# Placing the residual's border scale in the second mixing block, and later places for its side steps in TensorE's written order

## The chip, the core and the metric

The kernel runs on one core of one Trainium2 chip. The metric is the device time of one execution in microseconds, the median over runs. TensorE (PE in the profile) multiplies, VectorE (DVE) and GpSimd (POOL) do elementwise work, ScalarE (ACT) evaluates functions and issues part of the DMAs, SyncE (SP) issues the rest of them.

## What is computed

Two models run one after the other over 512 tokens of width 1024, two layers each. Block 1 has latent attention, indexed sparse attention, retention and a squared-ReLU network; block 2 has a gated delta rule (GDN), a native sparse attention with three branches (NSA), a stick-breaking attention, a convolved gated network and a gated embedding. Between them stands a border: the output of block 1 is `rmsnorm(x, g_final)`, and that is at once the residual of block 2 and the input of block 2's first norm. Cut to this:

```python
x = first_block(...)            # ends with: return rmsnorm(x, g_final)
h = x                           # second_block
for i in range(2):
    hn = rmsnorm_2(h, ln_mix[i])
    mix = concatenate([o_gdn, head_rmsnorm(o_nsa), head_rmsnorm(o_sb)])
    h = h + mix @ w_out[i]
    h = h + conv_ffn(rmsnorm_2(h, ln_ffn[i]), ...)
    h = h + sigmoid(rmsnorm_2(h, ln_ple[i]) @ w_ple_gate[i]) * rmsnorm_2(p[i] @ w_ple[i], ple_norm[i])
return rmsnorm_2(h, ln_final)
```

## The kernel before, in words

The residual x is kept in eight tiles of 128 features by 512 tokens (`x[k]`). Each float32 product is made as three products of a high and a low part (`mm3`, `mm3t`, line 382), so that weights are split after loading into `whi` (ACT, line 278) and `wlo` (DVE, line 279), and activations into `hi` and `lo`.

**TensorE's order is written out ahead.** While the program is built, `drive` keeps a plan clock `pe["t"]` that counts columns over 2400, in microseconds. A main thread (projections and output products) and side threads (attention heads, transposes, the delta rule, norms) yield lags: `yield 3.92` or `after(lag, "s")` means that the thread's next step isn't placed before so much plan time has passed and, for `after`, before a PSUM bank of that kind counts as free. When no thread is due, the plan clock jumps; on the chip nothing is waited for on that account, only the order is kept. `mark(name, lag)` sets a time from which `until(name)` holds. A side step that is due goes ahead of the main thread as the shares (`SHARE`) allow. PSUM banks of kind "s" (in block 2's mixing five, numbers 2 to 6) go round in strict rotation, those of kind "g" (two) likewise. The order on the other engines comes from the compiler's schedule, in which a step written earlier goes first where both are ready.

**Mixing of block 2** (`block2_mix`, line 1330). `norm` (line 1338) sums the squares over TensorE and makes the token scales `r`, then `rb`, their broadcast. The main thread goes through projections `kz`, the three feature projections of the delta rule (`delta(j)`, each three tiles, `post_g` at 1479), and the token projections between them; then `z`, `sq`, `sk`, `sv`. `post_g` convolves on DVE, transposes (`conv`), normalises q and k heads into `ghat` on POOL, and transposes these back (line 1515). `gdn_inverse` (line 1537) makes the 64x64 triangular systems: products kT kT, a product with `dts` on DVE into `lt`, transposes of `lt`, and DMAs through DRAM (`lsc`, `tsc`) from SP's queue; `gdn_solve` and `gdn_scan` follow. `keys` and `queries` turn NSA's keys and queries (`kwr`, `nq`) into high and low halves; `compress` makes the compressed keys and values from a "g" bank that its tail (`chid`) frees. `nsa` runs 48 heads in four workers; its result is transposed by `mix_features` (tile `on`), which ends in a mark from which the main thread takes up `out_proj(mixa)`. `breaking` (line 1990) makes the halves of `sq` and `sk` (tiles `q`, `k`, `kl`) and then runs the stick-breaking heads, whose first step (`weigh`) is products of `k` and `kl` with `q`.

**The residual in the mixing.** `put_away` writes the eight tiles of x to DRAM from ACT's queue, `fetch` reads them back ahead of `out_proj`, whose `post` adds to `x[m]`. In the first layer (`st["acc2"]` is there) `norm` also makes `rf`, the border norm's token scale; it broadcasts it (`rbf`), waits for the mark `dts`, and multiplies the eight tiles on DVE ahead of `put_away` (lines 1363 to 1368), the first of them behind the gates' last step (`steps[0]`).

In block 1's mixing the diff touches two lags: the one ahead of the indexer's scores (`qst`, line 924) and the mark of the rotated query part (`qr`, line 1029), from which `mla_queries` takes it up.

Of the kernel before, what the change touches and what calls it, by code (L numbers as in the profile page):

```python
# [9 lines left out]
F = mybir.dt.float32  # L10
# [279 lines left out]
def build(ctx, tc, a, out, off, stages=99):  # L290
# [550 lines left out]
    def block1_mix(l, st, nxt):  # L841
# [47 lines left out]
        def indexing():  # L889
            yield until("mi")  # L890
            yield after(0, "t")
            kst = sl([128, S], "kst", dt=R)
            tp = ps("t")
            for b in range(4):
                tr(tp[0:96, blk(b)], kx[b // 2][:, b % 2, 0:96])
            act(kst[0:96], tp[0:96])
            yield after(0, "t")
            kd.extend(key_halves([kx[b // 2][:, b % 2, 160:224] for b in range(4)], 1))
            yield after(0, "t")
            tp = ps("t")  # L900
            for b in range(4):
                tr(tp[0:32, blk(b)], kx[b // 2][:, b % 2, 128:160])
            act(krt[64:96], tp[0:32])
            mark("krt", 1.0)
            for b in (3, 2, 1):

                src = heads(qi[b // 2][:, b % 2], 8)
                hi = tmp([128, 8, 32], "qih", dt=R)
                act(hi, src)
                part = [tmp([128, 4, 3, 32], "qp") for _ in range(2)]  # L910
                for j in range(2):
                    z = slice(4 * j, 4 * j + 4)
                    nc.gpsimd.tensor_copy(out=part[j][:, :, 0:2], in_=hi[:, z].unsqueeze(2).to_broadcast([128, 4, 2, 32]))
                    tt(part[j][:, :, 2], src[:, z], hi[:, z], ALU.subtract)
                yield 4.75
                qst = []
                for j in range(2):
                    yield after(0, "t")
                    tp = ps("t")
                    for h in range(4):  # L920
                        tr(tp[0:96, blk(h)], part[j][:, h].rearrange("p t d -> p (t d)"))
                    qst.append(sl([128, S], "qst", dt=R))
                    act(qst[j][0:96], tp[0:96])
                yield after(0.98, "s")
                n = 128 * (b + 1)
                acc = None
                for h in range(8):
                    sp = ps("s")
                    mm(sp[:, 0:n], qst[h // 4][0:96, blk(h % 4)], kst[0:96, 0:n])
                    e = tmp([128, n], "rel")  # L930
                    act(e, sp[:, 0:n], ACTF.Relu)
                    new = tmp([128, n], "acc")
                    if acc is None:
                        ts(new, e, wi[:, b, h:h + 1], 0.0, ALU.mult, ALU.add)
                    else:
                        stt(new, e, wi[:, b, h:h + 1], acc, ALU.mult, ALU.add)
                    acc = new
                    yield after(0.36 + 0.2 * b, "s")
                begin(top(b, acc), 0)
                yield until(f"mask{b}")  # L940
# [78 lines left out]
        for c in range(3):  # L1019
            def post_q(b, p, c=c):  # L1020
                if c < 2:
                    act(qn[b][:, 256 * c:256 * c + 256], p[:, 0:256], scale=rq_[:, b:b + 1])
                else:
                    act(qr[b], p[:, 0:256], scale=rq_[:, b:b + 1])
                    rope(heads(qr[b], 8), heads(qr[b], 8), 8, 32, rope32, b)

            yield from token_proj(cq, 256, post_q, kt=6, need="rq_")
            if c:
                mark("qn" if c == 1 else "qr", 1.0 if c == 1 else 4.5)
        vm, kn, kT = [None] * 4, [None] * 4, []  # L1030

        def mla_keys():
# [297 lines left out]
    def block2_mix(l, st, nxt, shared):  # L1330
# [3 lines left out]
        r = const.tile([128, 4], F, tag="rmix", name="rmix")  # L1334
        r8 = const.tile([128, 4], F, tag="r8", name="r8")
        rb = sl([128, S], "rb")

        def norm():
            yield 3.92
            if st["acc2"] is None:  # L1340
                with tc.high_priority():
                    rms_cols(st["acc"], D, r)
                mark("r")
                ts(r8, r, 0.125)
                put_away()
            else:

                with tc.high_priority():
                    rf = rms_cols(st["acc"], D)
                    v = ty([128, 4], "border")  # L1350
                    stt(v, col_sums(st["acc2"]), 1.0 / D, rf, ALU.mult, ALU.mult)
                    tt(v, v, rf, ALU.mult)
                    ts(v, v, EPS, op0=ALU.add)
                    pow_half(v, v, 4)
                    tt(r, v, rf, ALU.mult)
                mark("r")
                ts(r8, r, 0.125)
            yield NR
            with tc.high_priority():
                bcast(r, rb)  # L1360
            mark("rb")
            if st["acc2"] is not None:
                rbf = bcast(rf)
                yield until("dts")
                for k in range(8):
                    ins = stt(x[k], x[k], P("g_final")[:, k:k + 1], rbf, ALU.mult, ALU.mult).ins
                    tc.add_manual_dep(ins, steps[0], NOSYNC, reason="the gates first")
                put_away()

        begin(norm(), 0)  # L1370
# [6 lines left out]
        beta, sig = gb("beta"), gb("sig", 18)  # L1377
        eG, eR, bG = gb("eG"), gb("eR"), gb("bG")
        eT = const.tile([128, 3, 4, 2], F, tag="eT", name="eT")
        dts, steps = [], []  # L1380

        ab = const.tile([128, 4, 30], F, tag="ab", name="ab")

        def gates():
# [37 lines left out]
            act(eG, p[:, 0:24].rearrange("p (b h) -> p b h", b=4), ACTF.Exp)  # L1422
            act(eR, p[:, 24:48].rearrange("p (b h) -> p b h", b=4), ACTF.Exp)
            act(eT.rearrange("p j b c -> p (j b c)"), p[:, 48:72], ACTF.Exp)
            steps.append(tt(bG, beta, eG, ALU.mult).ins.name)

            for h in range(6):
                tgs = [None, None]
# [50 lines left out]
        def post_g(i, p):  # L1479
# [21 lines left out]
            if what == 2:  # L1501
                for hh in range(2):
                    tt(B[2 * j + hh][:, :, 0:64], t4[:, :, hh], beta[:, :, 2 * j + hh:2 * j + hh + 1].to_broadcast([128, 4, 64]), ALU.mult)
            else:
                sq, t = tmp([128, 4, 2, 64], "gsq"), tmp([128, 4, 2, 64], "ghat")
                act(sq.rearrange("p b h d -> p (b h d)"), tp, ACTF.Square)
                act(t.rearrange("p b h d -> p (b h d)"), tp)
                n = ty([128, 4, 2], "gn")
                reduce(n, sq, ALU.add)
                ts(n, n, EPS, op0=ALU.add)  # L1510
                pow_half(n, n, 8)
                if what == 0:
                    ts(n, n, 0.125)
                gt(t, t, n.unsqueeze(3).to_broadcast([128, 4, 2, 64]), ALU.mult)
                yield after(PG[1], "t")
                (qT if what == 0 else kT)[j] = transposed([flat(t, b) for b in range(4)])
                if what == 0:
                    gt(t, t, per_token(eG, j, 64), ALU.mult)
                    yield after(2.0, "t")
                    WQ[j] = sl([128, 4, 2, 2, 64], "wq", "wq")  # L1520
                    tp = ps("t")
                    for b in range(4):
                        tr(tp[:, blk(b)], flat(t, b))
                    t4 = tp.rearrange("p (b c t) -> p b c t", b=4, c=2)
                    for ch in range(2):
                        act(WQ[j][:, :, ch, 1 - ch], t4[:, :, ch])
                else:
                    for hh in range(2):
                        h = 2 * j + hh
                        KA[h] = sl([128, 4, 2, 64], "KA")  # L1530
                        gt(KA[h][:, :, hh], t[:, :, hh], eR[:, :, h:h + 1].to_broadcast([128, 4, 64]), ALU.mult)
                        gt(B[h][:, :, 64:128], t[:, :, hh], bG[:, :, h:h + 1].to_broadcast([128, 4, 64]), ALU.mult)
# [4 lines left out]
        def gdn_inverse(j):  # L1537

            lt, L, T = [], [], []
            for hh in range(2):  # L1540
# [5 lines left out]
                    mm(p[:, blk(b)], kT[j][zz, blk(b)], kT[j][zz, blk(b)])  # L1546
                lt.append(tmp([128, S], "lt"))
                tt(lt[hh], p, dts[h], ALU.mult)
            yield 1.0
            for hh in range(2):  # L1550
                h = 2 * j + hh
                yield after(0, "t")
# [140 lines left out]
        def compress(kind):  # L1693
# [11 lines left out]
                    if c % 2:  # L1705
                        yield
            begin(compress_out(kind, p))
            room[0] = pe["t"] + 3.0

        def compress_out(kind, p):  # L1710
            hid, th = tmp([128, 128], "chid"), tmp([128, 128], "cth")
# [49 lines left out]
            roped(nq[0][:, b], b, p[:, 128:256], r8[:, b:b + 1])  # L1761

        yield from token_proj(xx, 256, post_v2)
        spawn(keys("kw", kwr), 9.05)
        spawn(queries(0), 16.9)
        yield from delta(2)
        spawn(compress_blocks(kcr, "k"), until("kc"), 0)
# [24 lines left out]
        def mix_features(o, i):  # L1792
            for k in range(3):
                yield after(0, "t")
                mixa[3 * i + k] = to_features([o[b][:, 2 * k:2 * k + 2].rearrange("p h d -> p (h d)") for b in range(4)], mixn[:, i:i + 1])
            mark(f"mix{i}", 2.28)

        def gdn_scan():
            yield until("rules")
# [129 lines left out]

        def sparse():  # L1930
            yield until("ks", "kw", "nq0", "nq1", "nq2", "vs", "cmp_k", "cmp_v")
            crew(LIVE[2], nsa(), "nsa", lag=8.62)
            yield until("nsa")
            yield from mix_features(on, 1)

# [70 lines left out]
            mark("mixb", 1.5)  # L2006

        begin(breaking())
        yield until("mix0", "mix1")
        fetch()  # L2010
        share(SHARE[4])
        yield from out_proj(mixa)
        yield until("mixb")
# [181 lines left out]
```

## Time and profile before

| | |
|---|---|
| median of 3 runs | 3048.47 us (3047.78 to 3053.13) |
| the profiled execution's own time | 3049.75 us |
| its span, first to last instruction | 3048.0 us |
| busy: PE, PEld, DVE, ACT, POOL | 97%, 81%, 62%, 45%, 23% of the span |
| mean granted clock of TensorE | 0.988 of full speed |
| DMA | 259.38 MB, mean 85 GB/s |

PE is TensorE's matmuls, PEld its weight loads, which lie beside them. A line of a wait names the instruction that stood still, what it waited for, the sum, how often and the longest. A line of a stretch has the length, then each engine's busy time with the number of instructions, the granted clock (1.00 is 2.4 GHz, 0.50 is 1.2 GHz), the DMAs' share and GB/s.

### The profile page before, as it was taken

To read this page: it belongs to the slowest core of one execution; us is meant where nothing else is said; L and a number is where in the kernel's file an instruction comes from. 1 tells how busy PE (TensorE), PEld (TensorE's weight loads), DVE (VectorE), ACT (ScalarE), POOL (GpSimd) and SP (SyncE) were. 2 spreads that over 40 slices of the span, in tenths; PEclk is the share of its full clock that TensorE was granted. 3 is DMA by queue.
4 is the path that set the end of the run, shared out by engine and by line. 5 is a ranking of instruction groups with operands and counts; after the bars stand their busy time and mean duration, and the time that the engine had idled before them with its cause. 6 is when DMAs were issued, how large, how long until landed. Compare 5 with 4: busy or idle time off the path is not lost.

```text
span 3048.0 us, 46930 instructions
## 1 busy us (share of the span) xinstructions
PE 2962.5 (97%) x18306; PEld 2472.4 (81%) x18306; DVE 1889.6 (62%) x3432; ACT 1360.6 (45%) x2536; POOL 713.6 (23%) x874
## 2 busy tenths in 40 slices
PE   8999999999999999998999999999999999999998
PEld 7888888888887888887898778887788987788876
DVE  6858444447858434457866675655778666755556
ACT  5644422244645332254455543334454565533343
POOL 4211311123201211145313120003454131200024
PEclk9999999999999999999999999999999999999999
DMA  4211223332122333322310222232323102222322
GB/s 135 77 62 58 86 94 97 97 117 84 64 77 73 97 92 95 97 92 91 89 58 24 82 91 94 92 106 90 115 78 87 60 24 80 92 92 94 106 90 76
DMA packets 105790, 259.38 MB, mean 85 GB/s; under 512 B 21728, under 2 KB 40032, under 8 KB 105568
## 3 DMA queue, kind: packets, MB, share of 16 engines
q1 hardware_dynamic: 97504, 241.70, 25.3%
q10 hardware_dynamic: 8064, 14.68, 1.4%
q8 instruction: 144, 2.36, 0.3%
q14 instruction: 78, 0.64, 0.1%
HBM read 242.84 MB, written 13.50 MB: 84 GB/s over the span
## 4 chain that ended last, share of the span: by engine, by line
PE 45%; DVE 6%; ACT 2%; issue 1%; POOL 1%; DMA 1%; DVEq 0%; POOLq 0%; SPq 0%; ACTq 0%
PE ps_g L382 36%; PE ps_s L382 5%; PE ps_s L392 2%; PE ps_o L388 2%; DVE wlo L279 1%; PE ps_s L388 1%; DVE conv L362 1%; POOL ru L354 1%; DVE kl L351 0%; DMA ll<-lsc 0%; ACT whi L278 0%; DVE pr L351 0%; DVE x L362 0%; DMA lsc<-L 0%; DVE inv L365 0%
## 5 line engine op out<-in xcount | busy, mean ns | idle before, releaser
L382 PE MATMUL ps_g<-hi,whi 128*128 128x512 f32 x2768 | 1097.9, 397 | 8.0 <-DVE x L351 3.5
L382 PE MATMUL ps_g<-lo,whi 128*128 128x512 f32 x2768 | 1094.8, 396 | 5.9 <-DVE lo L362 5.5
L382 PE MATMUL ps_g<-hi,wlo 128*128 128x512 f32 x2768 | 1096.0, 396 | 0.0
L278 ACT ACTIVATE whi<-wraw 128x1024 fp32r<-128x1024 f32 (+3 forms) x442 | 458.0, 1036 | 861.7 <-PE ps_g L382 611.0
L279 DVE TENSOR_TENSOR wlo<-wraw,whi 128x1024 fp32r<-128x1024 f32 (+3 forms) x442 | 548.7, 1241 | 250.5 <-ACT whi L278 247.3
L382 PEld LDWEIGHTS ps_g<-hi,whi 128*128 128x128 f32 x2768 | 522.2, 189 | 132.3 <-DVE x L351 6.8
L382 PEld LDWEIGHTS ps_g<-lo,whi 128*128 128x128 f32 x2768 | 522.6, 189 | 126.5 <-DVE lo L362 6.2
L382 PEld LDWEIGHTS ps_g<-hi,wlo 128*128 128x128 f32 x2768 | 522.3, 189 | 115.6
L382 PE MATMUL ps_g<-whi,hi 128*128 128x256 f32 (+4 forms) x1232 | 379.9, 310 | 18.4 <-ACT whi L278 9.0
L382 PE MATMUL ps_g<-whi,lo 128*128 128x256 f32 (+4 forms) x1232 | 348.0, 284 | 2.1 <-DVE lo L362 2.1
L382 PE MATMUL ps_g<-wlo,hi 128*128 128x256 f32 (+4 forms) x1232 | 347.7, 284 | 0.7 <-DVE wlo L279 0.7
L382 PEld LDWEIGHTS ps_g<-whi,hi 128*128 128x128 f32 (+1 forms) x1232 | 233.7, 190 | 35.6 <-ACT whi L278 9.4
L382 PEld LDWEIGHTS ps_g<-wlo,hi 128*128 128x128 f32 (+1 forms) x1232 | 233.4, 189 | 2.6 <-DVE wlo L279 1.0
L382 PEld LDWEIGHTS ps_g<-whi,lo 128*128 128x128 f32 (+1 forms) x1232 | 231.9, 188 | 4.4 <-DVE lo L362 2.9
L354 POOL TENSOR_TENSOR sq<-sq 128x512 f32<-128x512 f32 x102 | 158.5, 1554 | 268.7 <-ACT sq L337 249.9
L354 POOL TENSOR_TENSOR relu<-relu 128x512 f32<-128x512 f32 x64 | 100.9, 1577 | 506.5 <-ACT relu L337 506.5
L362 DVE SCALAR_TENSOR_TENSOR conv<-cv,small,conv 128x512 f32<-128x512 f32 x230 | 182.1, 796 | 5.8 <-ACT conv L337 2.4
L351 DVE TENSOR_TENSOR cv<-ps_g,rb 128x512 f32<-128x512 f32 x106 | 72.8, 690 | 144.0 <-PE ps_g L382 144.0
L351 DVE TENSOR_TENSOR x<-ps_g,x 128x512 f32<-128x512 f32 x112 | 76.9, 688 | 133.9 <-PE ps_g L382 133.0
L337 ACT ACTIVATE e<-ps_s,nm 128x128 f32<-128x128 f32 (+3 forms) x192 | 100.3, 525 | 110.6 <-DVE nm L365 107.3
L351 DVE TENSOR_TENSOR ff<-ps_g,rb 128x512 f32<-128x512 f32 x64 | 44.2, 691 | 162.9 <-PE ps_g L382 162.9
L2028 POOL MEMSET cv<- 128x2 f32 x88 | 8.7, 99 | 562.0 <-DVE conv L362 555.6
(432 smaller groups left out, 3708.6 us busy)
## 6 DMA issues: line engine op xcount, KB each, us to landing
wraw<-in_w_ff SPq DMA_DIRECT2D x128, 512.0 KB, 3.6
wraw<-in_w_up SPq DMA_DIRECT2D x88, 512.0 KB, 3.4
wraw<-in_w_down SPq DMA_DIRECT2D x32, 448.0 KB, 3.3
wraw<-in_w_out SPq DMA_DIRECT2D x20, 512.0 KB, 3.6
wraw<-in_w_g SPq DMA_DIRECT2D x18, 512.0 KB, 3.4
wraw<-in_w_down SPq DMA_DIRECT2D x16, 512.0 KB, 3.5
wraw<-in_w_pg SPq DMA_DIRECT2D x16, 512.0 KB, 3.4
wraw<-in_w_cq SPq DMA_DIRECT2D x12, 512.0 KB, 3.5
```

Of the source, the lines that this page charges most:

```text
L278: self.nc.scalar.activation(out=hi, in_=t, func=ACTF.Copy)
L279: self.nc.vector.tensor_tensor(out=lo, in0=t, in1=hi, op=ALU.subtract)
L337: ins = nc.scalar.activation(out=out, in_=in_, func=func, **kw).ins
L351: return nc.vector.tensor_tensor(out=out, in0=in0, in1=in1, op=op)
L354: return nc.gpsimd.tensor_tensor(out=out, in0=in0, in1=in1, op=op)
L362: return nc.vector.scalar_tensor_tensor(out=out, in0=in0, scalar=scalar, in1=in1, op0=op0, op1=op1)
L382: placed(nc.tensor.matmul(out=out, lhsT=lhsT, rhs=rhs, start=start, stop=stop).ins, n)
L388: placed(nc.tensor.matmul(out=out[z], lhsT=lhsT[:, z], rhs=rhs, start=start, stop=stop).ins, n)
L392: placed(nc.tensor.transpose(out=out, in_=in_, identity=ident[0:n, 0:n]).ins, 256)
L2028: nc.gpsimd.memset(h[:, 0:2], 0.0)
```

## The change

The border scale is kept in a tile of its own (`rf`), the first layer's `norm` puts x away unscaled, and the scale is broadcast when the mixing's main thread has made its projections and applied to the eight tiles after they were fetched. Besides, lags become longer: that of the norm's sums (3.92 to 7.0, in block 2's second layer alone), and those of `qst`, `qr`, the second transposes of `post_g`, `lt`, the bank of `compress`, the keys `kw`, the marks `mix0` and `mix1`, and the mark `nsa`.

```diff
@@ block1_mix
-                yield after(0.98, "s")
+                yield after(1.7, "s")
...
-                mark("qn" if c == 1 else "qr", 1.0 if c == 1 else 4.5)
+                mark("qn" if c == 1 else "qr", 1.0 if c == 1 else 6.8)
@@ block2_mix, norm
+        shared_rf = []
...
-            yield 3.92
+            yield 7.0 if l else 3.92
...
-                    rf = rms_cols(st["acc"], D)
+                    rf = rms_cols(st["acc"], D, const.tile([128, 4], F, tag="rf", name="rf"))
+                    shared_rf.append(rf)
...
             if st["acc2"] is not None:
-                rbf = bcast(rf)
-                yield until("dts")
-                for k in range(8):
-                    ins = stt(x[k], x[k], P("g_final")[:, k:k + 1], rbf, ALU.mult, ALU.mult).ins
-                    tc.add_manual_dep(ins, steps[0], NOSYNC, reason="the gates first")
                 put_away()
...
-            steps.append(tt(bG, beta, eG, ALU.mult).ins.name)
+            tt(bG, beta, eG, ALU.mult)
@@ post_g, gdn_inverse
-                yield after(PG[1], "t")
+                yield after(PG[1] + (3.0 if i == 0 else 0.7), "t")
...
-            yield 1.0
+            yield 2.0
@@ compress, keys, mix_features, sparse
-            room[0] = pe["t"] + 3.0
+            room[0] = pe["t"] + 4.5
...
-        spawn(keys("kw", kwr), 9.05)
+        spawn(keys("kw", kwr), 11.0)
...
-            mark(f"mix{i}", 2.28)
+            mark(f"mix{i}", 5.0)
...
-            crew(LIVE[2], nsa(), "nsa", lag=8.62)
+            crew(LIVE[2], nsa(), "nsa", lag=12.0)
@@ end of block2_mix
         begin(breaking())
+        rbf = bcast(shared_rf[0]) if shared_rf else None
         yield until("mix0", "mix1")
         fetch()
+        if rbf is not None:
+
+            for k in range(8):
+                stt(x[k], x[k], P("g_final")[:, k:k + 1], rbf, ALU.mult, ALU.mult)
         share(SHARE[4])
         yield from out_proj(mixa)
```

## Rows read from the trace of the kernel before

**Rows 1.** The page, part 1: busy us, share of the span, instructions.

```profile
PE 2962.5 (97%) x18306; PEld 2472.4 (81%) x18306; DVE 1889.6 (62%) x3432; ACT 1360.6 (45%) x2536; POOL 713.6 (23%) x874
```

**Rows 2.** PE's waits over the span: us in total, times, longest.

```profile
PE ps_g L382 <- DVE lo L362: 7.6, 5, 2.8
PE ps_s L392 <- POOL ghat L354: 7.0, 4, 2.9
PE ps_g L382 <- DVE cv L351: 6.5, 1, 6.5
PE ps_s L388 <- POOL sq L354: 5.8, 2, 5.6
...
PE ps_s L392 <- DVE qr L351: 4.2, 2, 2.6
...
PE ps_g L382 <- DVE chid L362: 2.8, 2, 1.6
PE ps_s L392 <- DVE kwr L351: 2.5, 2, 1.8
PE ps_s L392 <- DVE lt L351: 2.3, 4, 0.9
...
PE ps_s L382 <- ACT qst L337: 1.0, 2, 0.5
```

**Rows 3.** Stretches of low clock behind the front waits (six, three shown, and their sum).

```profile
794.30:797.70 3.40, 3.40 (x10) 2.65 (x9) 3.33 (x6) 3.33 (x6) 3.03 (x4) 0.50 0.00 0
...
2200.60:2207.40 6.80, 4.21 (x30) 4.20 (x30) 2.31 (x7) 2.41 (x6) 2.28 (x2) 0.50 0.22 71
...
2306.40:2313.20 6.80, 6.80 (x26) 5.61 (x25) 5.98 (x13) 0.81 (x2) 0.10 (x1) 0.50 0.47 148
sum 30.70, PE 27.76 PEld 23.29 DVE 22.52 ACT 12.81 POOL 12.38; mean PE 4.63 PEld 3.88 DVE 3.75 ACT 2.14 POOL 2.06
```

**Rows 4.** The same work in block 2's two layers, kz to the first lt transposes.

```profile
1358.69:1437.35 78.66, 68.73 (x384) 58.02 (x383) 59.95 (x113) 42.43 (x84) 37.76 (x48) 0.91 0.26 88
2207.66:2277.30 69.64, 65.59 (x383) 55.33 (x381) 50.67 (x95) 40.15 (x75) 38.09 (x48) 0.98 0.21 69
```

**Rows 5.** DVE in order of time, first layer: the kept residual's scale, and a plain product.

```profile
1382.55 11.78 DVE L362 SCALAR_TENSOR_TENSOR x<-x,small,rb 128x512 f32<-128x512 f32 x8
1394.25 0.74 DVE L362 SCALAR_TENSOR_TENSOR conv<-cv,small,conv 128x512 f32<-128x512 f32 x1
```

**Rows 6.** Stretches: second norm's projection, first layer's mixing end, 1755 on, around lt.

```profile
2208.00:2216.00 8.00, 8.00 (x56) 7.64 (x55) 4.54 (x16) 5.11 (x15) 1.79 (x7) 1.00 0.22 66
...
1755.00:1775.00 20.00, 18.21 (x76) 13.65 (x76) 17.11 (x18) 11.42 (x18) 12.30 (x7) 1.00 0.26 79
1692.90:1700.30 7.40, 4.70 (x14) 3.49 (x13) 7.27 (x11) 4.16 (x7) 0.00 (x0) 0.73 0.65 217
1700.30:1708.80 8.50, 8.50 (x34) 7.17 (x33) 3.22 (x8) 3.59 (x10) 0.21 (x2) 0.69 0.25 76
2296.00:2312.00 16.00, 14.18 (x72) 11.17 (x71) 15.24 (x40) 4.78 (x7) 5.98 (x11) 0.82 0.43 122
```

**Rows 7.** POOL in order of time: the heads' products, key's and then query's.

```profile
1424.51 1.04 POOL L354 TENSOR_TENSOR ghat<-ghat,gn 128x512 f32<-128x512 f32 x1
1425.91 1.94 POOL L354 TENSOR_TENSOR ghat<-ghat,gn 128x512 f32<-128x512 f32 x1 [0.36 <-DVE gn L358]
```

**Rows 8.** PE in order of time at the end of the first layer's mixing.

```profile
1690.76 0.63 PE L392 MATMUL ps_s<-const,on 128*128 128x128 f32 x4 [1.57 <-DVE q L351]
...
1699.31 0.80 PE L382 MATMUL ps_g<-lo,whi 128*128 128x512 f32 x1 [2.70 <-DVE lo L362]
...
1700.33 0.31 PE L382 MATMUL ps_s<-k,q 128*128 128x128 f32 x1
```

**Rows 9.** DVE in order of time there.

```profile
1689.22 2.81 DVE L351 TENSOR_TENSOR q<-ps_s,q 64x512 fp32r<-64x512 f32 x4 [0.41 <-ACT q L337]
1692.86 5.61 DVE L351 TENSOR_TENSOR kl<-ps_s,k 64x512 fp32r<-64x512 f32 x8 [0.83 <-ACT k L337]
1698.50 2.07 DVE L362 SCALAR_TENSOR_TENSOR lo<-ps_s,small,hi 128x512 fp32r<-128x512 f32 x3
```

More of the change, by code (lines that the diff above doesn't have):

```diff
@@ L1379, in block2_mix @@
         eT = const.tile([128, 3, 4, 2], F, tag="eT", name="eT")
-        dts, steps = [], []
+        dts = []
         ab = const.tile([128, 4, 30], F, tag="ab", name="ab")
```

## The prediction

> **What bounds it now.** The page's busy shares come first: TensorE is busy in 2962.5 of 3048.0 us, VectorE in 1889.6 [rows 1]. So no other engine sets the time as a whole, and work taken off TensorE's order gives nothing unless TensorE stood still for it. The second view is TensorE's own waits. They are few, and most belong to steps that the plan put in too early: `ghat` 7.0 us in four waits, `cv` 6.5 in one, the sums `sq` 5.6 in one, `qr` 4.2, `chid` 2.8, `kwr` 2.5, `lt` 2.3, `qst` 1.0, and 2.7 and 2.8 of the 7.6 for `lo` [rows 2]. The third view is the granted clock. Behind the longer waits it shows 0.50, the lower of the two levels (1.2 of 2.4 GHz): six such stretches in the front parts hold 27.76 us of TensorE's work [rows 3], which at full clock would have taken half, so 13.9 us are lost there beside the waits themselves. Behind a single wait of 1.76 us inside 1755 to 1775 it stays at 1.00 [rows 6].
>
> **The scale of the residual, taken out of the front.** Eight multiplications held VectorE for 11.78 us, 1.47 each, where a product of the same shape behind them takes 0.74 [rows 5]; `cv`, which frees a "g" bank, stood behind them, and that is the wait of 6.5 us. What it cost in all is read from the second layer, which does the same work without them: 78.66 against 69.64 us [rows 4], so 9.0. The broadcast's two products only move (about 0.5 us, an estimate from 56 mostly half as wide products in 8 us [rows 6]). Gain **8.5**. The eight writes to DRAM leave ACT's queue earlier; ACT is busy in 42 of 79 us there [rows 4] and hides their issue.
>
> At its new place the scale needs `rf`'s broadcast (eight small ACT and DVE steps, two products ahead of the `sq` transposes), the fetch, and eight steps on VectorE, 5.9 us at 0.74 and 11.8 at 1.47 [rows 5]. I take the low end: GpSimd was busy beside the 1.47, as in the second layer's stretch (38.09 of 69.64 us [rows 4]), and is nearly idle (0.21 of 8.50) where they go, with VectorE at 3.22 of 8.50 [rows 6]. They are written behind the heads' first step, so the heads' scans go first; the first output tile needs x only after its 18 products. Cost **1**, bounds 0 to 11.8. The Trainium skill (SBUF — State Buffer, "SBUF: two separate sides") says that VectorE, with both inputs in SBUF, and a GpSimd step that reads SBUF exclude each other for whole instructions. By that rule the low end holds wherever GpSimd rests; by the 1.47 alone the sum would be 5.9 us worse.
>
> **The second layer's norm.** The sums come 3.08 of plan later. A kz product has 286 columns, 0.119 of plan, in steps of three, so 27 go ahead; at 0.14 us each (56 in 8 us [rows 6]) that covers 3.8 of the 5.6. About 1.8 us of idleness stay, between the 1.76 without a fall and the 2.6 with one (`qr`), so I count half of the 2.1 us that the low clock cost (4.21 of work at 0.50 [rows 3]). Gain **4.8**, bounds 3.8 to 5.9. Next in line is `r`; the banks that wait for it are needed 36 products later, so it is hidden.
>
> **Block 1.** `qr` waits 4.2 us, and 3.40 us ran at 0.50 behind it [rows 2, 3], so 1.7 more; 2.3 of plan is about 2.5 us of products, and the keys' transposes, which the heads need too, come later anyway. Gain **5.9**. `qst` waits 1.0 and is covered by 0.72: gain **1.0**. The top-k chain behind it moves too, but the sparse heads wait for the last projection.
>
> **ghat, kwr, lt.** Waits 7.0 + 2.5 + 2.3 = 11.8 us [rows 2], and the four other low stretches hold 27.76 - 3.40 - 4.21 = 20.15 us of work [rows 3], 10.1 lost: 21.9 together. The key's `ghat` is written at 1425.55, the query's only at 1427.85 [rows 7]; the key needs 0.7, the query 3.0, and that is how they are moved, with `delta(1)` ahead of them. Against the whole sum speaks VectorE: around `lt` it is busy in 15.24 of 16 us [rows 6], so more products there soon wait for VectorE. I count three quarters, **16.5**, bounds 10 to 21.9. The inverse's DMAs on SP's queue move along, and weights behind them are loaded two ahead. The chain to `mix0` grows by some 7 of plan, but NSA's chain ends it.
>
> **compress.** 2.8 us; a bank held 1.5 longer helps only where a side step is due: half, **1.4**, bounds 0 to 2.8.
>
> **The end of the mixing.** Here I expect no gain. The projections are used up when the `on` transposes come, so lag 12.0 for 8.62 changes nothing in the order: they wait for banks that the `q` halves hold (1.57 [rows 8]). The marks of 5.0 and the 12.0 do put the first four heads ahead of the output products: in plan time from the halves on, heads at 10.5, output at about 14. The heads need `kl` and, by rotation, banks that `lo` frees; VectorE makes `q`, `kl` and `lo` nearly without rest until 1700.57 [rows 9]. Before, twelve output products ran around that hole, and the heads began at 1700.33 [rows 8], for some 2 us. Now the heads go into it and the twelve products come after it: at 0.24 us (76 in 18.21 [rows 6]) 2.9, at half clock 5.8, so 0.9 to 3.8 lost. I take **-1.5** per layer, near the full clock because the products run on from there, -3 in all. Bounds per layer: -6.1 (the whole shift of 3.38 + 2.72), and +8.9 (2.7 for `lo`, 1.6 for `on`, and 0.27 of 7.4 us and 0.31 of 8.5 for the clock [rows 6, 8]).
>
> **Late next.** What stands behind the moved steps wasn't tuned for it. I take **-4** in all, one or two waits of half a microsecond to 0.9 (as `lt` [rows 2]) per layer; bounds 0 to -8.
>
> **Sum.** 8.5 - 1 + 4.8 + 5.9 + 1.0 + 16.5 + 1.4 - 3 - 4 = 30.1. The profiled execution took 3049.75 us, 1.75 around its span; less 30.1 it is 3019.7. The median stands 1.28 below that execution, so 3018.4.
>
> **The rivals.** *The end of the mixing gains as well.* If the compiler's order on VectorE puts `lo` ahead of `kl`, the 2.70 and its like vanish, with the clock behind them: the -3 turns into +17, 8.9 in one layer and nearly as much in the other, and the time is 2998. For it: VectorE has no other order forced on it; against it: `kl` is written first.
>
> *VectorE or banks hold TensorE, whatever the order.* VectorE at 15.24 of 16 us [rows 6] is the sign for it. Of the 25 us of the steps in block 1 and of ghat, kwr, lt and compress half comes back: 3031. The Trainium skill (Perfetto Trace Analysis, "Optimization Strategy") says that gaps which repeat can mean too little PSUM for the next tile. By that rule a wait on a bank is not moved away by a lag; the 1.57 behind `q` agrees, the `ghat` waits, which are for data, don't.
>
> *Slower: TensorE starves at the end of block 2's mixing.* Place: between the last projection and `out_proj(mixa)`, both layers. Price per layer: the whole hole of 7.4 us [rows 6], 6.1 of shift, and 3.4 for a further stretch at 0.50; twice, 34, and in the first layer 11.8 if the scaling stands ahead of the heads: 45.8 against 34.1 (the gains above less 4), so 3060. It decides as soon as the loss passes 34 us. Against it: after the heads' first step the output products fill the order to the end.
>
> *The change doesn't do what it says.* If most longer lags end in the same order, because nothing else is due in between, the waits stay, and only the scaling's way out of the front counts: 8.5 - 1, less 3 at the end and 4 for what is late next, 3048. Against it: in the front the main thread has products due at each of these points.
>
> **Numbers.** Forecast 0.45 (its own range 3008 to 3029), end gains too 0.15, VectorE bound 0.24, no effect 0.08, starving 0.08. The first three are faster by over 0.2% (6 us, about what a measurement of this kernel can tell): faster 0.84, same 0.08, slower 0.08. The range takes in the end's gains and the upper bounds of VectorE's case and leaves out starving and no effect: 2996 to 3042.
>
> **What would show it.** Right: no `cv` wait behind x in the first layer's front; that stretch near 70 us instead of 78.66; `sq` wait near 2; `ghat`, `qr`, `kwr`, `lt` waits near nothing and clock 1.00 behind them; the hole before the stick heads still there. Wrong: new waits on VectorE in those stretches as long as the old ones; `lo` gone at the end; the eight scalings ahead of the heads' scans, with TensorE waiting on `sg` or x.

## The result, and the profile after

The changed kernel is slower: 3076.28 us, the median of 5 runs (3072.48 to 3080.64), against 3051.02 for the kernel before in the same session (5 runs, 3047.78 to 3054.47). The ratio is 1.0085 with a 95% interval of 1.0074 to 1.0096, so 23 to 29 us. The profiled execution took 3072.48 us, its span is 3070.6, and the mean granted clock fell from 0.988 to 0.984.

First, TensorE's waits over the whole span of the changed kernel (us in total, times, longest), beside [rows 2]:

```profile
PE ps_s L382 <- DVE kl L351: 9.6, 4, 3.0
...
PE ps_s L382 <- DVE L L351: 9.1, 2, 5.2
PE ps_s L382 <- ACT dgh L337: 8.1, 2, 4.6
PE ps_s L392 <- DVE kl L351: 7.4, 2, 3.7
PE ps_s L392 <- DVE sg L351: 4.6, 4, 2.9
PE ps_s L392 <- ACT qT L337: 3.7, 3, 1.8
...
PE ps_s L388 <- POOL sq L354: 0.9, 2, 0.7
PE ps_s L392 <- POOL ghat L354: 0.9, 1, 0.9
...
PE ps_s L392 <- DVE qr L351: 0.7, 2, 0.5
```

What the change aimed at is gone or small: the wait of 6.5 for `cv` is gone, and in all `sq` went from 5.8 to 0.9, `ghat` from 7.0 to 0.9 and `qr` from 4.2 to 0.7. (Two waits of 1.0 and 1.1 ahead of the `ghat` transposes stand under another name, `cv`, in this view.) In their place stand six rows that weren't there before or were small: `kl` twice, `L`, `dgh`, `sg`, `qT`, together 42.5 us. TensorE's busy time is 2971.1 us, 8.6 more than in [rows 1] for the same products: part of them ran at the lower clock. The other 14.0 of the 22.6 us by which the span grew are TensorE's idle time (85.5 us before, 99.5 after).

Second, the time by stretches. The bounds are the first product of the gates' triangle (`g,const`), the first `lt` transposes, the first `k` product of NSA's heads (called NSA's start below), the first `sk` transposes and the next stage's broadcast. First layer of block 2, before and after, in the columns of [rows 4]:

```profile
1377.16:1437.35 60.19, 50.26 (x283) 42.11 (x283) 46.26 (x68) 28.92 (x50) 30.39 (x34) 0.89 0.28 97
1437.35:1553.33 115.98, 109.66 (x873) 101.68 (x871) 96.71 (x261) 50.59 (x104) 36.19 (x53) 0.97 0.34 97
1553.33:1686.92 133.59, 133.34 (x1478) 116.40 (x1478) 81.47 (x211) 76.19 (x228) 40.49 (x54) 1.00 0.08 25
1686.92:1783.83 96.91, 88.93 (x558) 70.19 (x557) 68.96 (x104) 54.30 (x111) 20.76 (x29) 0.95 0.27 85
```

```profile
1376.94:1430.18 53.24, 50.93 (x324) 43.53 (x324) 43.11 (x64) 31.25 (x54) 33.84 (x37) 1.00 0.24 75
1430.18:1550.61 120.43, 110.75 (x880) 103.91 (x878) 94.58 (x261) 49.66 (x102) 31.38 (x50) 0.94 0.32 90
1550.61:1690.05 139.44, 133.05 (x1434) 114.97 (x1433) 79.16 (x206) 80.24 (x241) 40.65 (x54) 0.96 0.08 26
1690.05:1794.28 104.23, 92.71 (x558) 72.75 (x558) 73.28 (x111) 52.94 (x105) 19.99 (x28) 0.89 0.24 75
```

The gain is there and is given back: 7.0 us won up to `lt`, then 4.5, 5.9 and 7.3 lost, and the clock shows it (0.89 to 1.00 in the first stretch, 0.95 to 0.89 in the last). The bounds are places in TensorE's order, and the order differs: the first stretch now holds 41 products more, the third 44 fewer. All stretches, from the same view:

| stretch | before | after | difference |
|---|---|---|---|
| block 1 and block 2's first norm | 1377.16 | 1376.94 | -0.2 |
| first layer's mixing (the four above) | 406.67 | 417.34 | +10.7 |
| first layer's network, second layer's norm | 441.91 | 447.15 | +5.2 |
| second layer's mixing | 396.96 | 404.01 | +7.0 |
| the rest | 425.30 | 425.16 | -0.1 |

The sum, 22.6 us, is the difference of the spans. Block 1 gained next to nothing, where 6.9 were forecast, and the second norm's stretch lost 5.2, where 4.8 were to be won. (The 0.2 us for block 1 are finer than two executions can tell: in the eleven profiled ones with block 1's lags as before, that first stretch took 1377.16 to 1380.81 us, in the three with them longer 1376.94 to 1378.25.)

Third, the new waits, each with the instruction that released it. The second pair of `lt` transposes of the first layer (PE, then DVE; start, length, and in brackets the idle time before it with its releaser):

```profile
1457.89 0.65 PE L392 MATMUL ps_s<-const,lt 128*128 128x128 f32 x4 [0.28 <-DVE lt L351]
1462.25 1.09 PE L392 MATMUL ps_s<-const,lt 128*128 128x128 f32 x4 [3.71 <-DVE kl L351]
...
1458.06 0.68 DVE L351 TENSOR_TENSOR lt<-ps_s,dt 128x512 f32<-128x512 f32 x1
...
1459.32 2.79 DVE L351 TENSOR_TENSOR kl<-ps_s,k 64x512 fp32r<-64x512 f32 x4
```

The data were ready at 1458.74. What TensorE waited for was the bank, the next in rotation, from which VectorE was still making NSA's key halves (`kl`) until 1462.11. A wait for data has become a wait for a bank. Later in the front it is the iterations X of one pair of heads, behind the next pair's `lt` transposes (PE, then DVE):

```profile
1500.11 2.05 PE L382 MATMUL ps_s<-X,M 128*128 128x128 f32 x8 [5.19 <-DVE L L351]
...
1499.29 1.28 DVE L351 TENSOR_TENSOR L<-ps_s,beta 128x512 f32<-128x512 f32 x2
```

At the second layer's norm it is the broadcast (ACT, then PE):

```profile
2228.93 0.22 ACT L337 ACTIVATE ghi<-g 128x24 fp32r<-128x24 f32 x1 [2.09 <-DVE g L362]
2229.05 1.26 ACT L337 ACTIVATE dgh<-const,rmix 128x128 fp32r<-128x128 f32 x4
...
2230.37 0.80 PE L382 MATMUL ps_s<-dgh,ones_r 128*128 128x512 f32 x1 [4.55 <-ACT dgh L337]
2232.28 0.79 PE L382 MATMUL ps_s<-dgl,ones_r 128*128 128x512 f32 x1 [1.11 <-DVE dgl L362]
```

ScalarE's four small steps for the broadcast stand behind the gates' chain: ScalarE itself is idle for 2.09 us, waiting for `g`, and the broadcast's steps stand right behind `ghi` in its order.

At the end of the first layer's mixing (PE, then DVE) the stick-breaking heads stand at `kl`, and then at `sg` behind three of the eight scalings:

```profile
1697.26 0.44 PE L382 MATMUL ps_s<-k,q 128*128 128x128 f32 x1 [3.01 <-DVE kl L351]
...
1700.09 0.44 PE L382 MATMUL ps_s<-k,q 128*128 128x128 f32 x1 [2.04 <-DVE kl L351]
...
1709.00 0.48 PE L392 MATMUL ps_s<-const,sg 128*128 128x128 f32 x1 [2.89 <-DVE sg L351]
...
1694.32 5.62 DVE L351 TENSOR_TENSOR kl<-ps_s,k 64x512 fp32r<-64x512 f32 x8 [0.85 <-ACT k L337]
...
1706.69 2.05 DVE L362 SCALAR_TENSOR_TENSOR x<-x,small,rb 128x512 f32<-128x512 f32 x3
1708.66 0.28 DVE L351 TENSOR_TENSOR sg<-sg,rest 128x128 f32<-128x128 f32 x1
```

### The profile page after: what moved, and what is told of

It is laid out like the page before. It is cut to its first block, busy times and chain, and to the rows that moved or that the text cites. A ratio compares the mean times of both kernels' runs of the same rounds, so it can differ in the third digit from the quotient of the medians.

```text
span 3070.6 us, 46919 instructions
## 1 busy us (share of the span) xinstructions
PE 2971.1 (97%) x18304; PEld 2479.5 (81%) x18306; DVE 1885.8 (61%) x3437; ACT 1362.5 (44%) x2531; POOL 710.1 (23%) x874
## 4 chain that ended last, share of the span: by engine, by line
PE 45%; DVE 5%; ACT 2%; issue 1%; DMA 1%; POOL 1%; DVEq 0%; POOLq 0%; SPq 0%; ACTq 0%
PE ps_g L382 36%; PE ps_s L382 5%; PE ps_s L392 2%; PE ps_o L388 2%; DVE conv L362 1%; DMA lsc<-L 1%; DVE kl L351 1%; DMA ll<-lsc 1%; PE ps_s L388 1%; DVE wlo L279 1%; POOL ru L354 0%; ACT whi L278 0%; DVE pr L351 0%; ACT L337 0%; DVE L L351 0%
```

## The experiments

All are the kernel before with one part of the change, some with a correction beside it, or the changed kernel without a part; one has a lag of its own. Where a text below says how the written order differs, TensorE's products of the two traces were listed in the order of their starts and compared. In the sessions of the experiments the kernel before stood at 3050.26 to 3051.66 us. The theory at the start: each longer lag removes its own wait, but the order written behind it is another, and that order meets banks and orders of other engines that nobody placed it for. The rival: one part does harm by its own work (the scale at its new place, or the heads ahead of the output products), and the rest gains as forecast.

**The scale alone.** Only the hunks on `rf`, `rbf` and the eight scalings (front of this document).

> The kernel before with the moved scale alone (rf kept, put away unscaled, broadcast and eight products after the fetch); no lag changed. Theory 'waits are exchanged' (each longer lag trades one wait for another, the scale itself is good): the first layer's front gains about 9 us, the new place costs 3 to 6 (a wait of some 3.5 for the broadcast, a few for sg), so 3 to 6 us faster than before, and no X,M or lt wait of over 2 us. Rival 'the moved scale is what costs' (its bank, its slot and its VectorE steps disturb the second half of the mixing): slower than before by 10 us or more, with the wait for dgh and the wait for sg as in the whole change.

3049.17 us, ratio 0.9995 (0.9986 to 1.0004): no difference. The first layer's stretches:

```profile
1378.94:1431.82 52.88, 48.76 (x284) 40.93 (x283) 38.83 (x59) 29.13 (x50) 31.50 (x35) 0.94 0.20 66
1431.82:1548.42 116.60, 110.09 (x872) 101.72 (x871) 95.32 (x261) 50.84 (x104) 36.18 (x52) 0.97 0.33 96
1548.42:1685.68 137.26, 134.96 (x1481) 117.19 (x1481) 82.90 (x211) 79.84 (x241) 41.59 (x54) 1.00 0.08 25
1685.68:1784.91 99.23, 90.59 (x559) 71.40 (x557) 72.38 (x112) 52.78 (x108) 19.73 (x28) 0.93 0.27 84
```

7.3 us are won in the first stretch, and 0.6, 3.7 and 2.3 are lost in the others, though the scaling has work only in the last. What reaches the others is the order: two products of 512 columns less stand in the plan of the front, 0.43 us of plan time, so every step behind them is placed against another clock. The next run tests that.

**The scale with the order held.** The same, and the plan clock keeps the 0.43 us where the products stood and gives it back where they stand now. Between the two places the order is that of before; in the two traces, too, TensorE's products stand in the same order but for these two.

```diff
             if st["acc2"] is not None:
+                pe["t"] += 1024 / 2400
                 put_away()
...
         rbf = bcast(shared_rf[0]) if shared_rf else None
+        if shared_rf:
+            pe["t"] -= 1024 / 2400
```

> The moved scale alone again, but with the plan clock put forward by the two products that left the front and back by them where they now stand, so that TensorE's order is that of before apart from these two products. Theory 'a new order brings new waits': with the order held the 8.5 us that the front gains stay until the end of the first layer's mixing, less 1 to 3 for the new place: 5 to 8 us faster than before, and no wait of 1.5 us at wtok nor of 1 us at et, which came in with the moved scale alone. Rival 'the gain is given back anyway, because the sparse heads are bound by VectorE and ScalarE': within 2.5 us of before, with the front faster by 8.5 and the sq and sk transposes by less than 4.

3042.58 us, ratio 0.9967 (0.9955 to 0.998): 7.8 us faster than before, close to the 7.5 that was forecast for the scale (8.5 less 1). The first layer's second to fourth stretches now take 116.33, 135.14 and 97.08 us. The interval of the gain is 6 to 14 us. So the scale's own work is as forecast; what ate the gain was the new order, from a shift of 0.43 us of plan.

**The norm and block 1.** The lags 7.0 (second layer's sums), 1.7 (`qst`) and 6.8 (`qr`).

> The kernel before with three lags alone: the second layer's norm sums 7.0, qst 1.7, qr 6.8. Theory 'waits are exchanged': the norm's broadcast then waits behind the gates on ScalarE, so about 5 us slower there (between the sums and the gates' products), and block 1 unchanged within 1 us: 4 to 6 us slower in all. Rival 'the waits go': about 11 us faster. If the norm's new wait is an effect of other edits, the sums' part gains 4 and the total is some 4 faster.

3052.71 us, ratio 1.0009 (1.0000 to 1.0019): of the 11.7 us that were forecast nothing, and a loss of 2.5 that is hardly clear of noise (4 to 6 were expected of the exchanged waits). The broadcast waits 4.57 and 1.11 us, much as in the changed kernel (4.55 and 1.11). In block 1 the `qr` waits fall from 4.2 to 1.1 us in all, and the next transposes (`vm`) wait 1.75 in each layer for the bank from which ScalarE copies `qT` (eight copies, 4.80 us).

**The norm with its broadcast.** The lag of the sums is 7.0 in the second layer, and the lag behind it, ahead of the broadcast, is shorter by the same 3.08.

```diff
-            yield 3.92
+            yield 7.0 if l else 3.92
...
-            yield NR
+            yield NR - 3.08 if l else NR
```

> The kernel before with the second layer's norm sums at 7.0 of plan, and the broadcast's lag behind them shortened by the same 3.08 (8.0 to 4.92), so that the broadcast is written where it was written before. Theory 'the broadcast went behind the gates on ScalarE because it was written later': the dgh wait of 4.6 us and the dgl wait of 1.1 don't come, the sums' wait falls from 5.4 to about 1 or 2, and the stretch from the end of the layer before to the gates' products is 3 to 6 us shorter than in the kernel before; 3 to 5 us faster in all. Rival 'the sums themselves come too late for ScalarE': the dgh wait stays at 3 us or more and the total is within 2 us of before or slower.

3046.00 us, ratio 0.9983 (0.9973 to 0.9992): 4.4 us faster, against 4.8 forecast. In TensorE's order only the 16 products of the sums stand elsewhere than before. The sums wait 0.73 us, and the broadcast doesn't wait. ACT, then PE:

```profile
2208.14 0.68 ACT L337 ACTIVATE dgh<-const,rmix 128x128 fp32r<-128x128 f32 x2
...
2208.97 0.69 ACT L337 ACTIVATE dgh<-const,rmix 128x128 fp32r<-128x128 f32 x2
...
2205.98 0.63 PE L388 MATMUL ps_s<-const,sq 128*64 128x1 f32 x16 [0.73 <-POOL sq L354]
...
2213.65 0.40 PE L382 MATMUL ps_s<-dgh,ones_r 128*128 128x512 f32 x1
```

`dgh` is made by 2209.7, four us ahead of its product and well ahead of the gates. The harm lay not in the later sums but in the later broadcast that hung on them.

**The end of the mixing alone.** Marks of 5.0 for 2.28, and NSA's lag 12.0 for 8.62.

> The kernel before with the two marks at the end of block 2's mixing alone: mix0 and mix1 5.0, nsa 12.0. Theory 'waits are exchanged': the stick heads' first step goes ahead of the output products and waits for kl and banks (2 to 3 us twice per layer), the output products come later and stay over after the heads: 3 to 4 us slower per layer, 6 to 8 in all. Rival 'the order there hardly matters, VectorE sets the time': within 2 us of before. The reading of the planner that more plan time gives less waiting: 5 to 10 us faster.

3056.08 us, ratio 1.0017 (1.0007 to 1.0026): 5.8 us slower, about 3 per layer where 1.5 were forecast. The heads wait 2.55 and 2.03 us for `kl` in each layer, where the changed kernel has 3.01 and 2.04 in the first and 2.55 and 2.04 in the second.

**The front's lags.** `ghat`, `lt`, `compress` and `kw` together.

> The kernel before with the four lags of block 2's front alone: ghat 3.0 and 0.7, lt 2.0, the compress bank 4.5, kw 11.0. Theory 'waits are exchanged': the ghat waits go, a wait for kl at lt of over 3 us and one for L at X,M of over 3 us come in each layer, and the total is 0 to 15 us slower. Rival 'the waits go and the losses come from the other edits': 15 us faster or more, without these two waits.

3073.80 us, ratio 1.0074 (1.0059 to 1.0089): 23.5 us slower, more than either expectation had. The waits for `kl` and `L` came as expected; those for `ghat` didn't go (5.5 us in all, 4.7 of it in the second layer). This group carries the loss. Added up, the four groups come to 30.7 us (-1.1, +2.5, +5.8, +23.5), the whole change to 25.3.

**ghat alone, and kw alone.**

```diff
-                yield after(PG[1], "t")
+                yield after(PG[1] + (3.0 if i == 0 else 0.7), "t")
```

> The kernel before with the lags of ghat alone (3.0 and 0.7). Theory 'waits are exchanged': the 2.94 at ghat falls to about 1 in each layer, and the later systems bring new waits at X,M (for L) of 2 us or more; within 5 us of before either way, more likely slower. Rival 'it is kw that does the harm': 5 to 9 us faster, as the trace of before had it for ghat alone (7.0 of waits, 3.4 of clock).

3080.65 us, ratio 1.0094 (1.0078 to 1.0109): 30 us slower, more than the whole change, and far from both expectations. The waits for `ghat` fall only from 7.0 to 4.5 us (two more of 1.1 stand under `cv`). In the edit `i` counts the nine feature tiles: the 3.0 goes to the first pair's query alone, the 0.7 to all others.

> The kernel before with the lag of kw alone (11.0). Theory 'the keys' bank is what lt waits for': the kwr wait goes, the wait for kl of 3.7 us at lt comes in both layers, and it is 1 to 4 us slower. Rival 'kw alone is harmless, the two collide only when lt comes later too': no kl wait, 2 to 6 us faster.

`kw` alone: 3053.17 us, ratio 1.0006 (0.9997 to 1.0015). The `ghat` waits of before grow from 7.0 to 15.6 us in all without a measurable loss, and `lt` doesn't wait for `kl`; that wait needs another of the front's lags as well. In TensorE's order only the four `kwr` transposes of each layer have changed places with products of the main thread.

With ghat alone the first layer's stretches are these, and under them TensorE's waits from the first `lt` on. Then come the second layer's stretch from `lt` to NSA's start, before and with ghat alone, and the two longest waits from there on:

```profile
1378.12:1437.51 59.39, 51.22 (x315) 43.84 (x315) 49.59 (x72) 30.51 (x53) 32.78 (x37) 0.94 0.31 107
1437.51:1563.56 126.05, 113.71 (x883) 105.83 (x881) 95.54 (x261) 49.54 (x103) 32.73 (x51) 0.93 0.30 86
1563.56:1695.95 132.39, 129.60 (x1436) 111.91 (x1436) 75.15 (x199) 77.64 (x230) 39.42 (x53) 1.00 0.08 25
1695.95:1795.69 99.74, 87.76 (x558) 69.80 (x557) 69.15 (x106) 54.84 (x112) 21.60 (x30) 0.93 0.25 83
...
PE ps_s L392 <- DVE on L351: 8.6, 1, 8.6
PE ps_g L382 <- DVE wlo L279: 3.2, 1, 3.2
PE ps_s L392 <- DVE lt L351: 3.0, 2, 2.8
PE ps_g L382 <- ACT vw L337: 2.5, 1, 2.5
```

```profile
2277.30:2395.89 118.59, 113.71 (x908) 105.70 (x906) 97.61 (x263) 51.85 (x106) 35.12 (x52) 0.97 0.33 99
...
2289.65:2420.69 131.04, 112.59 (x882) 103.91 (x881) 95.88 (x261) 49.35 (x103) 35.31 (x51) 0.95 0.27 81
...
PE ps_s L392 <- DVE wtok L351: 4.0, 1, 4.0
PE ps_s L392 <- POOL ghat L354: 3.7, 1, 3.7
```

The loss lies between `lt` and NSA's start: 10 us in the first layer (126.05 against 115.98) and 12 in the second (131.04 against 118.59), 22.5 of the 29.0 us between the two profiled executions. It is TensorE's idle time above all (the stretch less the busy time: 6.3 to 12.3 us, and 4.9 to 18.5), spread over several waits, and in the first layer a lower clock as well (0.97 to 0.93). NSA starts the later for it, and its own length stays (132.39 against 133.59 in the first layer). At the end NSA is then late for the projections: its last normalised tile (`on`) was ready ahead of the halves before (1688.26, the halves from 1689.22), and now comes behind the halves `q` and half of `kl` on VectorE, and TensorE stands for 8.57 us in the first layer (PE, then DVE). Of this little is left in the time: that last stretch is 2.8 us longer than before, and in the second layer the wait for `on` is 0.6, as before.

```profile
1705.89 2.18 PE L392 MATMUL ps_s<-const,on 128*128 128x128 f32 x9 [8.57 <-DVE on L351]
...
1698.25 2.79 DVE L351 TENSOR_TENSOR q<-ps_s,q 64x512 fp32r<-64x512 f32 x4 [0.88 <-ACT q L337]
...
1705.28 0.56 DVE L351 TENSOR_TENSOR on<-on,hv 128x384 f32<-128x384 f32 x1
```

**ghat later, the inverse's mark earlier.** The theory after ghat alone: the cost comes from the chain that hangs on the tiles' mark (a pair's inverse and its solve), not from the transposes.

```diff
-                mark(f"tiles{j}", 1.0)
+                mark(f"tiles{j}", 1.0 - (3.0 if j == 0 else 0.7))
```

> Only ghat's lags are longer (3.0 and 0.7 of plan), but the mark from which a pair's inverse may start is set earlier by as much, so the inverse stands where it stood. Theory (the 30 us that ghat alone cost come from the inverse chain that starts later): the ghat waits stay at about 1 us each as in the run with ghat alone, and the 30 us go: 3036 to 3050. Rival (the transposes themselves, or the new order around them, cost it): 3065 to 3085 as with ghat alone.

3066.24 us, ratio 1.0052 (1.0038 to 1.0065): 15 us slower, between the two. The edit doesn't put the inverse back where it was, though. A mark can't hold before it is set, and it is set once the later transposes are placed; of the first pair's 3.0 us of plan only the 1.0 that the mark had comes back. The traces agree: the first pair's inverse begins with the 255th product of the first layer's stretch in the kernel before, with the 288th with ghat alone and with the 276th here. The stretch up to the first `lt` transposes has 283, 315 and 303 products:

```profile
1380.00:1438.42 58.42, 50.37 (x303) 42.83 (x302) 48.14 (x70) 29.49 (x51) 31.77 (x35) 0.94 0.31 106
```

So about half of ghat's cost goes when part of the chain's delay is taken back. Whether the other half is the rest of that delay, the transposes or the new order around them stays open. In its trace the long waits are `on` 8.6 in the first layer once more, and `kl` in both, 3.1 and 4.5, now ahead of the `conv` transposes. Which of these carries the rest wasn't tried.

**A lag of 0.1.** `yield 1.1` for `yield 1.0` ahead of the `lt` transposes: meant as an order that is merely another.

> The lag ahead of the transposes of lt is 1.1 in place of 1.0: of no use by itself, but the order that is written out changes in several places behind it. It shows how far an order that is merely another moves the time. If what counts is which step is pushed later, it is within 3 us of the kernel before (3047 to 3053). If any new order brings waits of its own of the size seen (8 to 30 us), it is 3058 or more.

3048.49 us, ratio 0.9991 (0.9981 to 1.0000). No loss. But in its trace TensorE's order is that of before except for three products in each layer, which stand 37 and 25 places earlier, so it shows only that such a small change can be free. With ghat alone some 1280 of the 18306 products stand elsewhere (by the shortest difference between the two lists). That a new order of that size costs by itself, whatever was moved, isn't ruled out; against it speaks the next run, where some 820 stand elsewhere at a loss of 6 us. And the `ghat` waits went from 7.0 to 13.2 us in this run, at no loss: a sum of waits that grows doesn't yet say that the time does.

**The change without ghat.**

> The whole change without the longer lags of ghat. Theory (ghat's later place pushes the inverse and all that hangs on it later, and that alone carries the loss): 26 less the 30 that ghat cost alone, so 3045 to 3051, the NSA's transposes (on) without a wait of 8 us, NSA's first product some 10 us earlier than in the changed kernel. Rival (any group of longer lags pushes the front into the same waits, ghat is one of several): 3060 to 3070, with waits for kl, X and on as in the changed kernel.

3057.48 us, ratio 1.0020 (1.0011 to 1.0030). Between the two expectations: taking ghat's lag back takes 19 of the 25 us away, and in the profiled executions 13.2 of 14.9 us in the first layer's mixing (404.1 against 417.3). The rest of the change keeps 6 us of loss, about what the end of the mixing cost alone, and gives nothing. It keeps waits for banks as well: `kl` holds the `conv` transposes up for 5.1 us in each layer.

**Both repaired parts.** The scale with the order held, and the norm with its broadcast.

> The scale at its new place with the plan clock held (the order as before: alone 7.8 us faster), together with the second layer's sums 3.08 of plan later and its broadcast 3.08 earlier behind them (alone 4.4 us faster). If the two gains come from waits that are really gone, each in its own layer, they add: 12.2 us, 3038. If what a layer gains is given back behind it by later waits, less than the larger one and a half stays: 3042 to 3046. Waits: none for cv behind the scale in the first layer, none above 1 us at the second layer's sums.

3039.11 us (5 runs, 3037.57 to 3041.28), ratio 0.9961 (0.9947 to 0.9975): 12.6 us faster than before and faster than the changed kernel. The two gains, 7.8 and 4.4, add. Its waits, where `cv` is gone and `ghat` and `lo` stay:

```profile
PE ps_s L392 <- POOL ghat L354: 9.5, 5, 2.9
PE ps_g L382 <- DVE lo L362: 9.2, 7, 2.8
...
PE ps_s L392 <- DVE qr L351: 3.9, 2, 2.3
```

## Why the prediction was wrong

It said 3018.4 us, 2996 to 3042, faster with 0.84. Measured: slower by 25 us. By its own steps:

- *The scale of the residual* (8.5 less 1) was right in its own place and size: 7.8 with the order held. That its two products "only move" was wrong: 0.43 us of plan moved the order of the whole stretch between, and gave the gain back. In the full change the new place shows waits for more than 1 as well: the broadcast waits 3.5 us for ScalarE, and the first layer's heads 3.9 us for `sg`. The 3.5 come with ghat's lag (0.5 in the change without it, with the same marks); how isn't shown.
- *The second layer's norm* (4.8) was right for the sums (a wait of 0.7 for 5.6) and wrong at "Next in line is `r` ... so it is hidden". Next in line is the broadcast, whose lag counts from the sums; on ScalarE it fell behind the gates. 4.4 us came once the broadcast was kept in its place.
- *Block 1* (5.9 and 1.0) cut its waits (`qr` from 4.2 to 0.7) and won 0.2 us in the profiled execution, by the others hardly more than 1 or 2: the next transposes wait for the bank that `qT` holds, and products of 512 columns behind that wait take 0.63 us each for a while where 0.39 is usual, so the low clock of [rows 3] is still there.
- *ghat, kwr, lt* (16.5) is the step that failed, and it carries the result. In the changed kernel its waits did go. But "The chain to `mix0` grows by some 7 of plan, but NSA's chain ends it" put at nothing what the lag drags along: a pair's inverse and its solve hang on the tiles' mark. ghat's lag alone costs 30 us, most of it ahead of NSA's start, so NSA's own chain comes later too; in the whole change it costs 19 of the 25. About half goes when part of the chain's delay is taken back; how the rest comes about stays open. The bound of 10 to 21.9 had no loss in it. The full lag of `lt` wasn't tried alone; that of `kw` alone changed nothing that can be measured.
- *Late next* (-4, bounds 0 to -8) was the right heading and the wrong size. One or two waits of half a microsecond per layer were counted; there are six rows with 42.5 us in all. It was priced from the waits that stood in the order of before, which don't say what another order brings.
- *The end of the mixing* (-3) was right in sign and mechanism, holes and low clock in front of the heads, and about half the size (5.8).
- *compress* (1.4) wasn't tried alone.

Of the rivals, "VectorE or banks hold TensorE" named a kind of wait that came: `kl` ahead of `lt` is a wait for a bank that VectorE holds. By the Trainium skill's rule that was weighed there (Perfetto Trace Analysis, "Optimization Strategy"), gaps that repeat can mean too little PSUM for the next tile; the 3.71 us at `lt`, in both layers, agree. That these waits carry the loss isn't shown, and two runs speak against it: the change without ghat has 10.2 us of them ahead of the `conv` transposes and loses 6 us, ghat alone has no wait for `kl` there or at `lt` and loses 30. Its price let half of the gain come back and no more, so it stayed on the wrong side of zero. The rival that was slower had part of the loss in the right place: at the end of the mixing the whole change loses 7.3 and 3.6 us. The larger part lies in other stretches (5.2 from `lt` to NSA's start, 8.0 in NSA, 5.2 up to the second layer's mixing).

## What to carry to other kernels

In an order that is written out against a plan clock, a lag isn't a local edit: ask what counts its own lag from the moved step (here the broadcast from the sums, the inverse from the tiles' mark), and price that chain before the wait that is removed. A wait for data that comes back as a wait for a bank (at `lt` 0.9 us became 3.71) can be looked for ahead by writing down, at the new place, which engine holds the next bank in rotation and what stands ahead of that step on it. When an edit takes work out of such an order, hold the order with a compensating term first (7.8 us for the one here), and only then tune. And compare the order in an experiment's trace with that of before: two of the edits here moved less, or gave back less, than they were written for.

## What the runs showed that was not expected

A shift of 0.43 us of plan, two products, decided over 6.6 us of time (ratios 0.9995 and 0.9967 for the same work). Waits that grew by 6 and by 9 us in sum (`ghat`, in the runs with 0.1 of lag and with `kw` alone) left the time where it was. And the eight scalings took 0.72 to 0.75 us each at their new place, beside a GpSimd that was busy in 0.21 of 8.60 us (order held), as the low end of [rows 5] had it, against 1.47 before.
